# Softmax and product with the values: two transfers taken out of the branches, and a load of 128 partitions cut into 104 and 24

## The chip, the cores and the metric

The kernel runs on one core of a Trainium2 chip. The metric is the device time of one execution in microseconds (us). A core has five engines with an instruction stream each: PE (TensorE, matrix products), DVE (VectorE), ACT (ScalarE), POOL (GpSimd) and SP (SyncE, which here issues every transfer). Transfers between the chip's memory and the core's on-chip memory are carried by 16 DMA engines. Engines wait for each other, and for transfers, by counting semaphores.

## The reference

```python
scores: (8, 12, 1024, 1024) float32      v: (8, 12, 1024, 64) float32
scores_max = np.max(scores, axis=-1, keepdims=True)
attn = np.exp(scores - scores_max)
attn = attn / (np.sum(attn, axis=-1, keepdims=True) + 1e-8)
return np.matmul(attn, v).astype(np.float32)
```

There are 96 heads. Each has 4 MB of scores, 256 KB of values and 256 KB of results.

## The kernel before, in words

A head is 1024 rows of scores. Each of the 128 partitions holds 8 of them, so one load of a head is 128 x 32 KB. The kernel works on *groups* of four heads (`AHEAD = 4`) in a loop of 24 turns, with one buffer of scores (`s_bufs`) for each head of a group. For each head k and each row r = 0 to 7:

- ACT takes the exponential of two rows at a time (L256, no maximum is subtracted). The last two rows of head 3 go one by one. So a head is four ACT instructions, head 3 is five.
- PE transposes the row in eight blocks of 128 x 128 (L268), and DVE copies the result out of PE's accumulator memory (L274, `pt`).
- Two rows later (`LAG = 2`) `finish` multiplies the transposed row with the values on PE (L146). The values carry a column of ones, so the sum of the exponentials comes out beside the product. After four or eight rows `normalise` divides on DVE: a reciprocal (L125) and two products (L130) into `out_sb`. Because of the lag the last rows of a head are finished when the next head's first rows are through; after head 3 the rest is finished at once.

The values of a whole group are loaded as one transfer of 1 MB (`load_v`, L195), cast to half precision by POOL (`cast_v`, L202), and spread by DVE with 16 small copies for a group (`spread_v`, L206) into the tiles that PE reads: four at the start of the group for head 0, and twelve behind the copies of heads 0 and 1, for heads 1 to 3. The results of two heads are stored as one transfer of 512 KB (`store`, L162).

SP issues the transfers in the order of the program. `queue` chains them, so none overtakes another, and each waits first for what it needs: a load of scores for ACT to be done with the buffer, a store for DVE, a load of values for POOL. Before the loop there are the values of the first group, the scores of its four heads, and the values of the second group (L294). In the loop, turn n0 loads the scores of the next group. Load 0 (head 0 of the next group) stands in the loop's body with a condition. Everything else stands at the end of the body in `last` (L215), which has three branches:

- all groups but the last two: load 1, `short` (16 partitions of 4 bytes, into a tile that nothing reads), store 0 (heads 0 and 1), load 2, the values of the group after the next, load 3, store 2 (heads 2 and 3);
- the last group but one: load 1 in two halves, store 0, load 2 in two halves, a quarter of load 3, store 2, the other three quarters;
- the last group: the two stores.

A transfer signals its end on a semaphore. The framework that the kernel is written in has eight for transfers, and gives them to a program's transfers in turn, 0 to 7 and again, as they stand in the program; a full transfer adds 16. In the first branch load 1 has number 1, `short` 2, store 0 number 3, load 2 number 4, the values 5, load 3 number 6, store 2 number 7. In the second branch the halves of load 1 have 1 and 2, store 0 has 3, the halves of load 2 have 4 and 5, the first quarter of load 3 has 6, store 2 has 7, and the other quarters have 0, 1 and 2. Load 0 always has 0. All three branches must leave each semaphore at the same count, since a wait in the next turn names one number for all. Where a branch has fewer transfers on a semaphore than another, SP adds the missing 16 itself, after a wait that all earlier counts on it are in. In the first branch SP does that for number 1 ahead of load 1, for number 2 ahead of `short`, and for number 0 at the end of the branch.

Of the kernel before, what the change touches and what calls it, by code (L numbers as in the profile page):

```python
# [8 lines left out]
FP32 = mybir.dt.float32  # L9
# [5 lines left out]
def kernel(  # L15
# [6 lines left out]
    nc = tc.nc  # L22
    P = 128
# [4 lines left out]
    BH = B * H  # L28
    assert SQ % P == 0 and SK % P == 0
    R = SQ // P  # L30
# [5 lines left out]
    AHEAD = 4  # L36
    Q = P // AHEAD
    S = P // Q
    L = 4
    T = 2  # L40
# [7 lines left out]
    v_bh = v.rearrange("b h (i t) d -> (b h i) (t d)", i=Q)  # L48
# [6 lines left out]
    sb_pool = ctx.enter_context(tc.tile_pool(name="sbpool", bufs=1))  # L55
# [7 lines left out]
        out=order16[:].rearrange("p (t j) -> p t j", t=T),  # L63
        in_=ident32[:].rearrange("p (j t) -> p t j", t=T),
# [13 lines left out]

    s_bufs = buffers(sb_pool, AHEAD, [P, R, SK], FP32, "s_nat")
    v_sb = sb_pool.tile([P, C // L, S, L, D], FP32, name="v_sb")  # L80
    short = sb_pool.tile([16, 1], FP32, name="short")
    v_half = sb_pool.tile([P, C // L, S, L, D], FP16, name="v_half")
    p_bufs = buffers(sb_pool, 8, [P, EB, SK], FP16, "p_nat")
    pt_bufs = buffers(sb_pool, 4, [P, SK], FP16, "pt")
# [9 lines left out]
    def take(bufs):  # L94
        k = turn.get(id(bufs), 0)
        turn[id(bufs)] = k + 1
        return bufs[k % len(bufs)]
# [4 lines left out]
    def after(a, b):  # L102

        tc.add_manual_dep(
            a.ins,
            b.ins.name,
            mybir.DependencyInfo(mybir.DependencyClass.NoSync, mybir.DependencyReason.DATA),
            reason="order",
        )

    def queue(dma):

        if queued:
            after(dma, queued[-1])
        queued.append(dma)

    def one(bh, n):
        return bh[bass.ds(n, 1)].rearrange("o p r d -> (o p) r d")

    def normalise(k, st, first, last):  # L120

        psO = psO_whole if k % 2 == 0 else psO_banks[first]
        psO = psO[:, :, 0 : G * M].rearrange("p b (g m) -> p b g m", m=M)
        recip = st["recip"][:, first:last]
        nc.vector.reciprocal(out=recip, in_=psO[:, :, :, D : D + 1])  # L125
        h = k % T
        for t in range(T):
            part = slice(t * W, (t + 1) * W)
            rows = st["out_sb"][h * W : (h + 1) * W, t, first * G : last * G, :]
            nc.vector.tensor_tensor(  # L130
                out=rows.rearrange("j (b g) d -> j b g d", g=G),
                in0=psO[part, :, :, 0:D],
                in1=recip[part].to_broadcast([W, last - first, G, D]),
                op=mybir.AluOpType.mult,
            )

    def finish(u):

        n0, k, r, pt, st = u
        b, g = r // G, r % G  # L140
        if r == 0:
            st["recip"] = take(rc_bufs)
            st["out_sb"] = out_bufs[k // T]
        bank = psO_whole[:, b] if k % 2 == 0 else psO_banks[b][:, 0]
        for c in range(C):
            nc.tensor.matmul(  # L146
                out=bank[:, g * M : (g + 1) * M],
                lhsT=pt[:, c * P : (c + 1) * P],
                rhs=st["vones"][:, c, 0:M],
                start=(c == 0),  # L150
                stop=(c == C - 1),
            )
        if k % 2 == 1:
            if g == G - 1:
                normalise(k, st, b, b + 1)
        elif r == R - 1:
            normalise(k, st, 0, R // G)

    def store(n0, k):

        rows = out_bh.rearrange("(m x) y -> m x y", x=P)
        dma = nc.sync.dma_start(  # L162
            out=rows[bass.ds((n0 + k) // T, 1)].rearrange("o x y -> (o x) y"),
            in_=out_bufs[k // T][:].rearrange("x t r d -> x (t r d)"),
        )
        for other in stores:
            apart(dma, other)
            apart(other, dma)
        apart(dma, dma)
        stores.append(dma)  # L170
        queue(dma)
# [3 lines left out]
    def apart(dma, other):  # L175
        tc.declare_no_dep(
            dma.ins, other.ins, across_iterations=True, reason="stores of two heads are disjoint"
        )

    def load(k, n, parts=(R,), r=0, **cond):  # L180
        for rows in parts:
            queue(
                nc.sync.dma_start(
                    out=s_bufs[k][:, r : r + rows, :],
                    in_=one(sc_bh, n)[:, r : r + rows, :],
                    **cond,
                )
            )
            r += rows

    def load_v(n):

        rows = v_bh.rearrange("(m x) y -> m x y", x=P)
        queue(
            nc.sync.dma_start(  # L195
                out=v_sb[:].rearrange("x h s l d -> x (h s l d)"),
                in_=rows[bass.ds(n // AHEAD, 1)].rearrange("o x y -> (o x) y"),
            )
        )
# [4 lines left out]
    def spread_v(k, s, behind=None):  # L204

        copy = nc.vector.tensor_copy(  # L206
            out=vones_bufs[k][s * Q : (s + 1) * Q, :, 0:D].rearrange(
                "i (h l) d -> i h l d", l=L
            ),
            in_=v_half[k * Q : (k + 1) * Q, :, s],  # L210
        )
        if behind is not None:
            after(copy, behind)

    def last(n0):  # L215

        before = queued[-1:]

        with tc.If(n0 < BH - 2 * AHEAD) as cmp:
            queued[:] = before
            load(1, (n0 + (AHEAD + 1)) % BH)
            queue(nc.sync.dma_start(out=short[:], in_=v_bh[0:16, 0:1]))
            store(n0, 0)
            load(2, (n0 + (AHEAD + 2)) % BH)
            load_v((n0 + 2 * AHEAD) % BH)
            load(3, (n0 + (AHEAD + 3)) % BH)
            store(n0, T)
        with cmp.Else():  # L230
            with tc.If(n0 < BH - AHEAD) as cmp2:  # L231
                queued[:] = before
                load(1, BH - 3, (4, 4))
                store(n0, 0)
                load(2, BH - 2, (4, 4))
                load(3, BH - 1, (2,))
                store(n0, T)
                load(3, BH - 1, (2, 2, 2), 2)
            with cmp2.Else():
                queued[:] = before  # L240
                store(n0, 0)
                store(n0, T)

    def heads(n0):

        for k in range(AHEAD):
            if k == 0:
                for s in range(S):
                    spread_v(k, s)
            st = dict(vones=vones_bufs[k])  # L250
            for r in range(R):
                if r % EB == 0:
                    p_nat = take(p_bufs)
                    rows = 1 if k == AHEAD - 1 and r == R - EB else EB
                    for g in range(0, EB, rows):
                        nc.scalar.activation(  # L256
                            out=p_nat[:, g : g + rows, :].rearrange(
                                "p r (x v) -> p x r v", v=Q * L
                            ),
                            in_=s_bufs[k][:, r + g : r + g + rows, :].rearrange(  # L260
                                "p r (i x l) -> p x (r i) l", i=Q, l=L
                            ),
                            func=EXP,
                        )
                p_row = p_nat[:, r % EB, :].rearrange("p (h q l) -> p h l q", q=P, l=L)
                psT = take(psT_bufs)
                for c in range(C):
                    nc.tensor.transpose(  # L268
                        out=psT[:, c * P : (c + 1) * P],
                        in_=p_row[:, c // L, c % L, :],  # L270
                        identity=order16[:],
                    )
                pt = take(pt_bufs)
                copy = nc.vector.tensor_copy(out=pt[:], in_=psT[:])  # L274

                if k < 2 and r < 6:
                    spread_v(1 + (k * 6 + r) // S, (k * 6 + r) % S, copy)
                if k == 0 and r == R - 1:
                    load(0, (n0 + AHEAD) % BH, cond=n0 < BH - AHEAD)
                pending.append((n0, k, r, pt, st))  # L280
                if len(pending) > LAG:
                    finish(pending.pop(0))
        while pending:
            finish(pending.pop(0))
        cast_v()
        last(n0)

    assert AHEAD == 4 and T == 2 and R == 8
    assert BH % AHEAD == 0 and BH >= 2 * AHEAD and SK == Q * S * C
    load_v(0)  # L290
    for k in range(AHEAD):
        load(k, k)
    cast_v()
    load_v(AHEAD)  # L294
    with tc.For_i(0, BH, AHEAD, iteration_sync="reg_based") as n0:
        queued.clear()
        heads(n0)
# [30 lines left out]
```

## Time and profile before

| What | Value |
|---|---|
| median of three timed runs | 1087.0 us (1086.9 to 1087.21) |
| profiled execution | 1086.9 us, span from first to last instruction 1085.1 us |
| PE, DVE, ACT, POOL busy | 740.3, 786.5, 735.6, 48.1 us |
| exponentials of two rows (L256) | 408 instructions with the single rows, 704.8 us |
| copies of transposed rows (L274) | 768, 516.8 us, 686 ns each |
| spreads of the values (L206) | 384, 109.5 us, 285 ns each |
| casts of the values (L202) | 25, 47.4 us, 1896 ns each |
| DMA moved | 453.05 MB, mean 418 GB/s over the span |
| a load of scores, from issue to landing | 36.1 us median |
| mean granted clock of PE | 0.828 |

The span counts from the first instruction to the last; what lies around it makes the 1.8 us up to the execution's own time. In the page's slices each digit is the busy share of a fortieth of the span, in tenths. A row of a timeline gives the start, the length, the engine, the line and form, and, in brackets, how long the engine had been idle before it and what released it.

### The profile page before, as it was taken

To read this page: it belongs to the slowest core of one execution; us is meant where nothing else is said; L and a number is where in the kernel's file an instruction comes from. 1 tells how busy PE (TensorE), PEld (TensorE's weight loads), DVE (VectorE), ACT (ScalarE), POOL (GpSimd) and SP (SyncE) were. 2 spreads that over 40 slices of the span, in tenths; PEclk is the share of its full clock that TensorE was granted. 3 is DMA by queue.
4 is the path that set the end of the run, shared out by engine and by line. 5 is a ranking of instruction groups with operands and counts; after the bars stand their busy time and mean duration, and the time that the engine had idled before them with its cause. 6 is when DMAs were issued, how large, how long until landed. Compare 5 with 4: busy or idle time off the path is not lost. (4 is left out here: it accounts for less than half of the span.)

```text
span 1085.1 us, 32113 instructions
## 1 busy us (share of the span) xinstructions
PE 740.3 (68%) x12288; PEld 687.1 (63%) x12288; DVE 786.5 (72%) x1589; ACT 735.6 (68%) x432; POOL 48.1 (4%) x31
## 2 busy tenths in 40 slices
PE   2756776776767667768676767686766767766725
PEld 2756666666667666667676666676666666666625
DVE  3776876876868768678687686786876968768627
ACT  3766685866667767667677676685866666857625
POOL 0000000000000000000000000000000000000000
PEclk9887888878888888788888887888888878888768
DMA  9999999999999999999999999999999999999970
GB/s 405 424 420 427 432 436 426 436 431 429 432 435 424 443 428 432 435 427 430 440 425 436 432 428 429 438 428 438 429 429 440 426 435 434 428 436 434 422 302 39
DMA packets 25619, 453.05 MB, mean 418 GB/s; under 512 B 3472, under 2 KB 3472, under 8 KB 9616
## 3 DMA queue, kind: packets, MB, share of 16 engines
q1 hardware_dynamic: 25616, 453.00, 97.3%
q8 instruction: 3, 0.05, 0.0%
HBM read 432.01 MB, written 25.17 MB: 421 GB/s over the span
## 5 line engine op out<-in xcount | busy, mean ns | idle before, releaser
L256 ACT ACTIVATE p_nat<-s_nat 128x2048 f16<-128x2048 f32 (+1 forms) x408 | 704.8, 1800 | 246.8 <-DMA s_nat<-in_scores_dram 201.7
L268 PE MATMUL psT<-order,p_nat 128*128 128x128 f16 x6144 | 581.2, 248 | 273.4 <-ACT p_nat L256 269.7
L274 DVE COPY pt<-psT 128x1024 f16<-128x1024 f16 x768 | 516.8, 686 | 227.5 <-PE psO_whole L146 86.8
L268 PEld LDWEIGHTS <-p_nat 128*128 128x128 f16 x6144 | 451.9, 123 | 297.3 <-ACT p_nat L256 297.2
L146 PEld LDWEIGHTS <-pt 128*128 128x128 f16 x6144 | 307.5, 109 | 94.7 <-DVE pt L274 93.6
L146 PE MATMUL psO<-vones,pt 128*128 128x65 f16 x3072 | 183.6, 205 | 60.4 <-DVE pt L274 59.2
L146 PE MATMUL psO_whole<-vones,pt 128*128 128x65 f16 x3072 | 189.3, 211 | 5.0 <-DVE pt L274 3.9
L206 DVE COPY vones<-v_half 32x512 f16<-32x512 f16 x384 | 109.5, 285 | 23.0 <-POOL v_half L202 5.9
L202 POOL CAST v_half<-v_sb 128x2048 f16<-128x2048 f32 x25 | 47.4, 1896 | 1014.9 <-DMA v_sb<-in_v_dram 951.3
L256 ACT ACT_TABLE_LOAD x24 | 30.8, 1283 | 89.7 <-DMA s_nat<-in_scores_dram 81.7
L130 DVE TENSOR_TENSOR out_sb<-psO,recip 64x256 f32<-64x256 f32 x192 | 81.1, 423 | 6.0
L130 DVE TENSOR_TENSOR out_sb<-psO_whole,recip 64x512 f32<-64x512 f32 x96 | 66.0, 688 | 3.0
L125 DVE RECIPROCAL recip<-psO 128x4 f32<-128x4 f32 x96 | 17.4, 181 | 32.5 <-PE psO L146 17.6
L125 DVE RECIPROCAL recip<-psO_whole 128x8 f32<-128x8 f32 x48 | 9.7, 203 | 0.8
L71 DVE MEMSET vones<- 128x16 f16 x4 | 0.2, 72 | 0.8 <-PEq L312 0.8
L62 DVE CAST order<-ident 128x128 f16<-128x128 f32 x1 | 0.2, 227 | 0.4 <-POOL ident masks.py:199 0.4
masks.py:199 POOL TENSOR_SCALAR_AFFINE_SELECT ident<-ident 128x128 f32<-128x128 f32 x1 | 0.3, 293 | 0.1
masks.py:197 POOL MEMSET ident<- 128x128 f32 x1 | 0.2, 205 | 0.3 <-POOLq L312 0.3
L312 POOL MEMSET const-float32-0.0<- 128x1 f32 x1 | 0.1, 99 | 0.2 <-issue 0.2
L312 POOL MEMSET const-bfloat16-1.0<- 128x1 bf16 x1 | 0.1, 102 | 0.0
L312 POOL MEMSET const-uint8-127<- 128x1 uint8 x1 | 0.1, 102 | 0.0
L312 POOL MEMSET const-float32-1.0<- 128x1 f32 x1 | 0.1, 99 | 0.0
## 6 DMA issues: line engine op xcount, KB each, us to landing
s_nat<-in_scores_dram SPq DMA_DIRECT2D x94, 4096.0 KB, 36.1
v_sb<-in_v_dram SPq DMA_DIRECT2D x24, 1024.0 KB, 36.9
out_dram<-out_sb SPq DMA_DIRECT2D x48, 512.0 KB, 26.8
s_nat<-in_scores_dram SPq DMA_DIRECT2D x4, 2048.0 KB, 35.3
s_nat<-in_scores_dram SPq DMA_DIRECT2D x4, 1024.0 KB, 24.4
short<-in_v_dram SPq DMA_DIRECT2D x22, 0.1 KB, 35.7
```

Source lines behind the costliest of these rows:

```text
L62: nc.vector.tensor_copy(out=order16[:].rearrange("p (t j) -> p t j", t=T), in_=ident32[:].rearrange("p (j t) -> p t j", t=T),)
L71: nc.vector.memset(vo[:, :, D : D + 2], 1.0)
L125: nc.vector.reciprocal(out=recip, in_=psO[:, :, :, D : D + 1])
L130: nc.vector.tensor_tensor(out=rows.rearrange("j (b g) d -> j b g d", g=G), in0=psO[part, :, :, 0:D], in1=recip[part].to_broadcast([W, last ...
L146: nc.tensor.matmul(out=bank[:, g * M : (g + 1) * M], lhsT=pt[:, c * P : (c + 1) * P], rhs=st["vones"][:, c, 0:M], start=(c == 0), stop=(c ...
L202: nc.gpsimd.tensor_copy(out=v_half[:], in_=v_sb[:])
L206: copy = nc.vector.tensor_copy(out=vones_bufs[k][s * Q : (s + 1) * Q, :, 0:D].rearrange("i (h l) d -> i h l d", l=L), in_=v_half[k * Q : ( ...
L256: nc.scalar.activation(out=p_nat[:, g : g + rows, :].rearrange("p r (x v) -> p x r v", v=Q * L), in_=s_bufs[k][:, r + g : r + g + rows, :] ...
L268: nc.tensor.transpose(out=psT[:, c * P : (c + 1) * P], in_=p_row[:, c // L, c % L, :], identity=order16[:],)
L274: copy = nc.vector.tensor_copy(out=pt[:], in_=psT[:])
L312: nc = _bacc.Bacc("TRN2", target_bir_lowering=False, num_devices=1)
```

## The change

Load 1 and store 0 leave the branches. Load 1 now stands in the loop's body with a condition, as load 0 does, behind the last row of head 1 (`load_next`); store 0 is issued from `finish` when head 1 is done. `short` is gone. In the branch of the last group but one, load 3 comes in pieces of 4, 2, 1 and 1 rows, with the store behind the first piece, and load 1 comes whole. The twelve spreads of a group go behind every second row of heads 0, 1 and 2. The second load of values, ahead of the loop, becomes two transfers: partitions 0 to 103, and 104 to 127. The numbers of the transfers' semaphores change with the order of the program: load 0 has 0, load 1 has 1, store 0 has 2; in the first branch load 2 has 3, the values 4, load 3 has 5, store 2 has 6; in the second the halves of load 2 have 3 and 4, the first piece of load 3 has 5, store 2 has 6, and the other pieces have 7, 0 and 1; in the third store 2 has 3. What SP has to add by itself in the first branch (on 0, 1 and 7) now stands at its end.

```diff
--- before.py
+++ after.py
@@ -78,7 +78,6 @@
 
     s_bufs = buffers(sb_pool, AHEAD, [P, R, SK], FP32, "s_nat")
     v_sb = sb_pool.tile([P, C // L, S, L, D], FP32, name="v_sb")
-    short = sb_pool.tile([16, 1], FP32, name="short")
     v_half = sb_pool.tile([P, C // L, S, L, D], FP16, name="v_half")
     p_bufs = buffers(sb_pool, 8, [P, EB, SK], FP16, "p_nat")
     pt_bufs = buffers(sb_pool, 4, [P, SK], FP16, "pt")
@@ -155,6 +154,8 @@
                 normalise(k, st, b, b + 1)
         elif r == R - 1:
             normalise(k, st, 0, R // G)
+        if r == R - 1 and k == T - 1:
+            store(n0, 0)
 
     def store(n0, k):
 
@@ -212,34 +213,32 @@
         if behind is not None:
             after(copy, behind)
 
+    def load_next(k, n0):
+
+        if k < AHEAD - 2:
+            load(k, (n0 + (AHEAD + k)) % BH, cond=n0 < BH - AHEAD)
+
     def last(n0):
-
 
 
         before = queued[-1:]
 
         with tc.If(n0 < BH - 2 * AHEAD) as cmp:
             queued[:] = before
-            load(1, (n0 + (AHEAD + 1)) % BH)
-            queue(nc.sync.dma_start(out=short[:], in_=v_bh[0:16, 0:1]))
-            store(n0, 0)
-            load(2, (n0 + (AHEAD + 2)) % BH)
+            load(AHEAD - 2, (n0 + (2 * AHEAD - 2)) % BH)
             load_v((n0 + 2 * AHEAD) % BH)
-            load(3, (n0 + (AHEAD + 3)) % BH)
-            store(n0, T)
+            load(AHEAD - 1, (n0 + (2 * AHEAD - 1)) % BH)
+            store(n0, AHEAD - T)
         with cmp.Else():
             with tc.If(n0 < BH - AHEAD) as cmp2:
                 queued[:] = before
-                load(1, BH - 3, (4, 4))
-                store(n0, 0)
-                load(2, BH - 2, (4, 4))
-                load(3, BH - 1, (2,))
-                store(n0, T)
-                load(3, BH - 1, (2, 2, 2), 2)
+                load(AHEAD - 2, BH - 2, (4, 4))
+                load(AHEAD - 1, BH - 1, (4,))
+                store(n0, AHEAD - T)
+                load(AHEAD - 1, BH - 1, (2, 1, 1), 4)
             with cmp2.Else():
                 queued[:] = before
-                store(n0, 0)
-                store(n0, T)
+                store(n0, AHEAD - T)
 
     def heads(n0):
 
@@ -272,11 +271,10 @@
                     )
                 pt = take(pt_bufs)
                 copy = nc.vector.tensor_copy(out=pt[:], in_=psT[:])
-
-                if k < 2 and r < 6:
-                    spread_v(1 + (k * 6 + r) // S, (k * 6 + r) % S, copy)
-                if k == 0 and r == R - 1:
-                    load(0, (n0 + AHEAD) % BH, cond=n0 < BH - AHEAD)
+                if k < AHEAD - 1 and r % (R // S) == 0:
+                    spread_v(k + 1, r // (R // S), copy)
+                if r == R - 1:
+                    load_next(k, n0)
                 pending.append((n0, k, r, pt, st))
                 if len(pending) > LAG:
                     finish(pending.pop(0))
@@ -285,13 +283,19 @@
         cast_v()
         last(n0)
 
-    assert AHEAD == 4 and T == 2 and R == 8
     assert BH % AHEAD == 0 and BH >= 2 * AHEAD and SK == Q * S * C
     load_v(0)
     for k in range(AHEAD):
         load(k, k)
     cast_v()
-    load_v(AHEAD)
+
+
+    for part in (slice(0, 104), slice(104, P)):
+        queue(
+            nc.sync.dma_start(
+                out=v_sb[part].rearrange("x h s l d -> x (h s l d)"), in_=v_bh[P : 2 * P][part]
+            )
+        )
     with tc.For_i(0, BH, AHEAD, iteration_sync="reg_based") as n0:
         queued.clear()
         heads(n0)
```

## The prediction, made before the result was known

> **What bounds the kernel now.** I read the page's slices first, then busy time by stretches, then ScalarE's timeline and waits, SP's issues, and last the trace's records of single packets and completions.
>
> ```profile
> span 1085.1 us, 32113 instructions
> DMA  9999999999999999999999999999999999999970
> GB/s 405 424 420 427 432 436 426 436 431 429 432 435 424 443 428 432 435 427 430 440 425 436 432 428 429 438 428 438 429 429 440 426 435 434 428 436 434 422 302 39
> q1 hardware_dynamic: 25616, 453.00, 97.3%
> ```
>
> The sixteen DMA engines are full until about 1050 us; then they stand nearly idle for 35. Up to there only bytes per engine count; behind it the length of the tail does. The tail by stretches (columns: stretch, its length, busy time of PE, weight load, DVE, ACT, POOL, granted clock, DMA share, GB/s):
>
> ```profile
> 45.00:1005.00 960.00, 676.41 (x11230) 627.76 (x11228) 719.37 (x1451) 674.16 (x396) 43.62 (x23) 0.83 1.01 432
> 1029.70:1050.30 20.60, 3.55 (x60) 3.42 (x57) 4.07 (x8) 0.00 (x0) 0.00 (x0) 0.58 0.97 413
> 1050.30:1072.20 21.90, 17.31 (x316) 15.78 (x317) 17.12 (x34) 21.84 (x13) 1.90 (x1) 0.88 0.08 31
> ```
>
> For 20.6 us ScalarE does nothing while the loads run on; then it works 21.84 us without a pause while they don't. Compute that should have lain beside the last loads follows them. ScalarE's timeline (start, length, form, count, idle before and its releaser):
>
> ```profile
> 1010.12 7.42 ACT L256 ACTIVATE p_nat<-s_nat 128x2048 f16<-128x2048 f32 x5 [4.75 <-DMA s_nat<-in_scores_dram]
> 1021.03 1.28 ACT L256 ACT_TABLE_LOAD   x1 [3.49 <-DMA s_nat<-in_scores_dram]
> 1022.33 7.32 ACT L256 ACTIVATE p_nat<-s_nat 128x2048 f16<-128x2048 f32 x4
> 1050.31 21.84 ACT L256 ACTIVATE p_nat<-s_nat 128x2048 f16<-128x2048 f32 x13 [20.67 <-SPq L323]
> ```
>
> And its waits (total, times, longest):
>
> ```profile
> ACT p_nat L256 <- SPq L323: 44.9, 22, 20.7
> ```
>
> So 21 of these waits share 24.2 us (1.15 each, released with a landing), and one is 20.7: the last group's head 1. The completion records tell on what. The loads of that group land at (latest engine): load 0 1020.94; the halves of load 1 1025.78 and 1030.62; of load 2 1036.83 and 1041.68; the quarters of load 3 1044.10, 1047.78, 1050.21, 1052.63. Head 1 had its data at 1030.6, yet started 0.1 us after 1050.21: the third quarter of load 3. In the built program that quarter (second-last branch) shares semaphore 1 with load 1, and the wait of head 1 asks for the full 32 counts of a group on it, since in the first branch SP adds the spare 16 ahead of load 1's own. The stall is a shared counter, not missing data.
>
> **The change, part by part.**
>
> *Load 1 leaves the branches.* On semaphore 1 its 16 are now the first of each group; ScalarE's wait in the built program asks for 32n+16, where it asked for 32(n+1). The last row of load 3 also counts there, but second. The stall of 20.67 us goes. Late next is the data itself. In order, from the landings above: load 1 whole at 1030.6; head 1 runs 7.32 to 1038.0; head 2 has its first half since 1036.8, its second at 1041.7, just when two activations of about 1.83 are through, and ends at 1045.4. Load 3's first piece is now four rows: 1041.68 + 4.85 (what halves of load 2 are apart) = 1046.53. Behind it: store 1.24, two rows 2.44, one row 1.22, one row 1.22 (half of 2.43 each): the end at 1052.7. Head 3 starts at 1046.6 and takes 7.42; its rows 4 to 7 have landed at 1050.2, 1051.4, 1052.7, before they are needed (1050.3, 1052.1, 1053.1). So only the first piece holds it.
>
> *From head 3's start to the end.* VectorE's rows of the group before, whose head 3 started at 1010.12 with all data there, and those of the end:
>
> ```profile
> 1013.61 0.69 DVE L274 COPY pt<-psT 128x1024 f16<-128x1024 f16 x1 [4.45 <-PE psO_whole L146]
> 1023.83 0.88 DVE L130 TENSOR_TENSOR out_sb<-psO,recip 64x256 f32<-64x256 f32 x2
> 1079.56 0.88 DVE L130 TENSOR_TENSOR out_sb<-psO,recip 64x256 f32<-64x256 f32 x2
> ```
>
> 1023.83 + 0.88 - 1010.12 = 14.6 us from the first exponential to the last product. In the old tail, where ScalarE ran ahead, the same stretch from the first copy was 1070.37 to 1080.44 = 10.1, against 1013.61 to 1024.71 = 11.1; that 1.0 is the lower bound's gain. I take 14.6, as ScalarE is again fed piece by piece. From the last product to the span's end: 1085.1 - 1080.44 = 4.66 (store issued, landed at 1083.13, closing). Unchanged.
>
> *The second load of values.* An 8 KB packet takes 309 ns, starting about 3 ns before its forerunner ends: 8 x 0.306 = 2.45 us per engine and load. With three engines empty, thirteen share 128 packets; ten instead of eight on the fuller ones: +0.61 us. The trace shows no transfer of 104 partitions; bounds are 0 (as now) and 2.45 (the same again on some engine). I take 0.6, nearest to the count of packets. What it can bring: from 60 us on, three of the sixteen completions of every transfer come 2.3 to 2.5 us behind the other pack, after three 16 KB packets of the instruction queue at 27.1, 36.7 and 47.5 us (0.88 to 0.97 each). If those are the uppermost engines, they lose 2.45 and fall in with the rest. But a fourth engine, 0.5 late at 68 us, loses some 0.11 per group in the first store's packets and is last at the end: 2.88 behind the first at 1052.63, while the three are 2.27 to 2.41. The latest decides a landing, so the cut gains nothing unless that drift goes too. I keep the drift: gain 0, bound -2.4 (the pack ends at 1050.2).
>
> [...]
>
> *The 64 byte load goes*: 22 times a data packet and a completion packet of 9 ns on each engine, about 12 ns net of overlaps: -0.26.
>
> *Store 0 and load 1 issued outside the branch.* SP's order stays load 0, load 1, store 0, load 2, values, load 3, store 2; a skipped issue (0.34) in the last group is new. New on SP: at the end of each first branch it waits for load 1 of the same group. In the group before the last branches, head 0's exponentials end at 941.9, so load 0 went out at 942.18; load 1 landed at 943.1. So load 0 goes out 1.0 later, and behind it on SP all else. Cover: what is still queued then (load 2, values, load 3, store 2: 9.7 + 2.45 + 9.7 + 1.24 = 23 us). Cost 0. Without the cover it would be 22 x 1.0.
>
> *Spreads of the values* (384 x 285 ns, same number): 12 per group now behind every second copy of heads 0 to 2. The last comes about 2 us after head 2's exponentials; the cast (1.90) follows it rather than the landing, and the load of values behind the cast goes out some 3.3 later than the 0.69 after load 2 seen at 962.55 and 963.24. Load 3 waits for head 3's exponentials (973.86) anyway; under the same 23 us: 0. VectorE is 75% busy in the steady stretch, so the moved copies hide too.
>
> **Sum.** Head 3 starts at 1046.53 + 0.6 - 0.26 + 0.05 = 1046.9; + 14.6 = 1061.5; + 4.66 = 1066.2 span, 18.9 less. The profiled execution took 1086.9 for its span of 1085.1 (+1.8) and stands 0.1 under the median: 1066.2 + 1.8 = **1068.0**.
>
> **The rivals.**
> 1. *The drift goes as well* (its cause may be the three late engines). The pack alone then sets the landings: 1068.0 - 2.4 = 1065.6. For it: the lag grows only in one store per group. Against: it grew at the same pace at 0.5 late as at 2.2. 25%.
> 2. *The stall stays*: ScalarE or VectorE still waits for a whole counter, now ended by the last row at 1052.7. The old tail of 32.5 us behind the last landing gives 1087.3. Against: the count in the built program. 4%.
> 3. *Slower*: the new wait at the branch's end outlasts the queue. It decides when SP is held over 23 us past load 1's landing, that is if it has to wait for the group's last store. Then each of 22 groups starts on empty engines, at 2.35 (the first load took 4.8 us from issue for 2.45 of packets): +52, 1120. Against: it names load 1. 4%.
> 4. *Another wait takes part of the stall* (store 0's buffer, a late piece): 5 to 12 us of the 20.7 come back, 1073 to 1080. 7%.
>
> My forecast itself: 60%.
>
> **How the numbers follow.** Cases 0 and 1 hold 85%. Their bounds: 1065.6 less 1.0 (VectorE dense) and a little, 1064; 1068.0 plus 1.9 (split at its upper bound) and 2 for the tail's pieces, 1072. Some of that 85 lies outside: 8 in 10 inside. About 0.2%, 2 us, is what a measurement tells from no change: slower 5% (rival 3 and a little), same 4% (rival 2), faster 91%.
>
> **What would show it.** ScalarE: no idle of 20 us near 1030; head 1 of the last group starts at about 1031, released by its load; the last load lands within 3 us of 1052.7; the last product at 1061.5; 14.6 from head 3's start. Completions: three engines no longer 2.3 late. Wrong if ScalarE waits on a semaphore that SP raises, if the DMA row shows slices under 9 before 1040, or if the tail behind the last landing is much over 13 us.

## The result and the profile after

The changed kernel takes 1069.39 us (median; 1069.25 to 1070.48), the kernel before 1086.95 in the same comparison: a ratio of 0.9841 with a 95% interval of 0.9823 to 0.9858, 17.6 us less. The prediction was 1068.0 in a range of 1064 to 1072. The profiled execution took 1069.4, its span 1067.6, predicted 1066.2.

The page of the changed kernel, in the lines that were shown of the kernel before:

```profile
span 1067.6 us, 32186 instructions
DMA  9999999999999999999999999999999999999995
GB/s 393 380 431 433 432 432 432 428 436 431 434 432 432 432 432 432 432 432 429 435 431 433 432 432 432 428 436 431 433 432 432 432 430 433 432 432 429 435 431 215
q1 hardware_dynamic: 24777, 453.00, 99.1%
```

The engines are full until 1055 us and nearly idle for 12, no longer for 35. The second slice is slower than before (380 against 424); that comes back below. The first is too (393 against 405), but it is as low with the second load of values whole (394), so the cut has no part in it. Busy time by stretches of the same kernel (stretch, length, busy time of PE, weight load, DVE, ACT, POOL, granted clock, DMA share, GB/s):

```profile
45.00:1005.00 960.00, 668.53 (x11177) 619.79 (x11176) 717.10 (x1444) 671.44 (x395) 41.65 (x22) 0.84 1.01 431
1033.00:1049.20 16.20, 13.20 (x251) 11.47 (x247) 15.12 (x32) 14.66 (x9) 0.00 (x0) 1.00 0.99 423
1049.20:1062.40 13.20, 8.80 (x176) 7.69 (x176) 11.97 (x24) 7.51 (x5) 1.89 (x1) 0.95 0.33 136
```

The steady stretch is as it was. In the last group compute now lies beside the loads, and the busiest engine there is VectorE, at 15.12 of 16.2 us. ScalarE's timeline at the end:

```profile
1023.53 1.28 ACT L255 ACT_TABLE_LOAD   x1 [3.48 <-DMA s_nat<-in_scores_dram]
1024.82 7.32 ACT L255 ACTIVATE p_nat<-s_nat 128x2048 f16<-128x2048 f32 x4
1033.21 10.93 ACT L255 ACTIVATE p_nat<-s_nat 128x2048 f16<-128x2048 f32 x6 [1.07 <-DMA s_nat<-in_scores_dram]
1049.19 7.63 ACT L255 ACTIVATE p_nat<-s_nat 128x2048 f16<-128x2048 f32 x5 [1.12 <-DMA s_nat<-in_scores_dram]
```

Head 1 of the last group waits 1.07 us and is released by its own load; the wait of 20.67 is gone. So it is in ScalarE's waits, whose longest behind SP is now 1.1:

```profile
ACT p_nat L255 <- SPq L226: 23.7, 22, 1.1
```

VectorE's last row puts the last product's end at 1062.42:

```profile
1061.54 0.88 DVE L129 TENSOR_TENSOR out_sb<-psO,recip 64x256 f32<-64x256 f32 x2
```

The trace's completion records give the rest: the last row of load 3 lands at 1055.35, where the last quarter of load 3 of the kernel before landed at 1052.63. The end of the loads comes 2.7 us later, although no more bytes are moved.

### The profile page after: what moved, and what is told of

Its sections match the earlier page's. It is cut to its first block, busy times and chain, and to the rows that moved or that the text cites. A ratio compares the mean times of both kernels' runs of the same rounds, so it can differ in the third digit from the quotient of the medians.

```text
span 1067.6 us, 32186 instructions
## 1 busy us (share of the span) xinstructions
PE 731.7 (69%) x12288; PEld 677.4 (63%) x12288; DVE 786.5 (74%) x1589; ACT 735.7 (69%) x432; POOL 48.0 (4%) x31
## 4 chain that ended last, share of the span: by engine, by line
DMA 82%; ACT 12%; issue 3%; ACTq 1%; PE 0%; DVE 0%; SPq 0%; PEld 0%; DVEq 0%
DMA s_nat<-in_scores_dram 82%; ACT p_nat L255 12%; ACTq L255 1%; ACTq L226 0%; ACTq L299 0%; SPq L184 0%; DVE pt L273 0%; PE psO L145 0%; PE psT L267 0%; PEld L267 0%; ACTq L327 0%; DVE out_sb L129 0%; PE psO_whole L145 0%; SPq L196 0%; PEld L145 0%
## 5 line engine op out<-in xcount | busy, mean ns | idle before, releaser
L267 PE MATMUL psT<-order,p_nat 128*128 128x128 f16 x6144 | 574.3, 246 | 270.3 <-ACT p_nat L255 269.5
L267 PEld LDWEIGHTS <-p_nat 128*128 128x128 f16 x6144 | 446.7, 123 | 298.9 <-ACT p_nat L255 296.3
L145 PEld LDWEIGHTS <-pt 128*128 128x128 f16 x6144 | 300.8, 107 | 84.6 <-DVE pt L273 81.2
L145 PE MATMUL psO<-vones,pt 128*128 128x65 f16 x3072 | 176.9, 201 | 55.9 <-DVE pt L273 52.7
L203 POOL CAST v_half<-v_sb 128x2048 f16<-128x2048 f32 x25 | 47.3, 1893 | 1005.4 <-DVE vones L207 957.4
```

Source lines behind the costliest of these rows:

```text
L145: nc.tensor.matmul(out=bank[:, g * M : (g + 1) * M], lhsT=pt[:, c * P : (c + 1) * P], rhs=st["vones"][:, c, 0:M], start=(c == 0), stop=(c ...
L203: nc.gpsimd.tensor_copy(out=v_half[:], in_=v_sb[:])
L267: nc.tensor.transpose(out=psT[:, c * P : (c + 1) * P], in_=p_row[:, c // L, c % L, :], identity=order16[:],)
```

## The experiments

**Is the stall a shared counter?** The kernel before, load 1 still in the branches. Only the last three quarters of load 3 become one transfer, so that no piece of load 3 counts on the semaphore of load 1.

```diff
-                load(3, BH - 1, (2, 2, 2), 2)
+                load(3, BH - 1, (6,), 2)
```

> The kernel before, load 1 still in the branches; only the last three quarters of load 3 of the last group but one are one transfer of six rows, so that no piece of load 3 uses the semaphore of load 1. Theory C (the stall of 20.7 us is a shared counter): head 1 of the last group starts at about 1030.7, released by its own load; the six rows land at 1052.6, their exponentials take 5.6 more, and the products end 6 to 7 behind that, at 1064 to 1065.5; span 1069 to 1070.5, time 1071 to 1072.5. Rival (ScalarE waits for the end of load 3 as such, or for SP): the stall stays and is 2.4 us longer, time 1089.

1071.13 us (1070.65 to 1071.88), ratio 0.9855 (0.9838 to 0.9871): 15.8 us less by changing the pieces of a single load. ScalarE's timeline of this kernel:

```profile
1022.27 18.38 ACT L256 ACTIVATE p_nat<-s_nat 128x2048 f16<-128x2048 f32 x10
1041.79 5.52 ACT L256 ACTIVATE p_nat<-s_nat 128x2048 f16<-128x2048 f32 x3 [1.14 <-PE L268]
1052.86 5.61 ACT L256 ACTIVATE p_nat<-s_nat 128x2048 f16<-128x2048 f32 x4 [5.56 <-DMA s_nat<-in_scores_dram]
```

Head 1 follows head 0 without a gap (load 1 still comes in halves here, so it starts even before the expected 1030.7), and the only long wait is 5.56 for the six rows, which land at 1052.76. All 22 of ScalarE's waits behind SP are gone from its list; its waits for loads of scores number 71, where they numbered 49. The data and SP's order are those of before; what went is the count on one semaphore. That the stall was the shared counter is shown.

**What does the cut of the second load of values cost?** The changed kernel with that load whole, and the kernel before with the cut alone.

```diff
-    for part in (slice(0, 104), slice(104, P)):
-        queue(
-            nc.sync.dma_start(
-                out=v_sb[part].rearrange("x h s l d -> x (h s l d)"), in_=v_bh[P : 2 * P][part]
-            )
-        )
+    load_v(AHEAD)
```

> The changed kernel with the second load of values whole again. Theory S (the cut is what made the loads of scores land 2.7 us later than before, through packets that took 620 ns instead of 309): the packets of that load are back at 309 ns, the last row of load 3 lands at about 1052.4 instead of 1055.35, and the time falls by 2.5 to 3.0, from 1069.4 to 1066.4-1066.9. Rival L (the late landing comes from the third packet of the instruction queue, which now hits an engine of the pack): the last landing stays within 1 us of 1055.3 and the time within 1 us of 1069.4. Rival D (the cut pays, because three late engines are made up for): the time rises above 1070.

1065.59 us (1065.52 to 1066.29), ratio 0.9807 (0.9791 to 0.9824). The last row of load 3 lands at 1052.18. This version is 3.8 us faster than the changed kernel, 0.8 more than the most that was expected, and the fastest of the three.

```diff
-    load_v(AHEAD)
+    for part in (slice(0, 104), slice(104, P)):
+        queue(
+            nc.sync.dma_start(
+                out=v_sb[part].rearrange("x h s l d -> x (h s l d)"), in_=v_bh[P : 2 * P][part]
+            )
+        )
```

> The kernel before with the cut of the second load of values alone. Theory S: ScalarE's stall in the last group stays (some 20 us, ended by the third quarter of load 3), and that quarter lands 2.4 to 3.0 later than 1050.2; time 1089.4 to 1090. Rival D (the cut pays): 1084 to 1086. Rival: it makes no difference, 1086.9 within 0.7.

1089.76 us (1089.55 to 1089.95), ratio 1.0027 (1.0016 to 1.0038): 2.9 more. The stall is there, and its end has moved from 1050.31 to 1053.09:

```profile
1053.09 7.32 ACT L256 ACTIVATE p_nat<-s_nat 128x2048 f16<-128x2048 f32 x4 [20.70 <-SPq L328]
```

So the cut costs 2.9 us in the kernel before and 3.8 in the changed one. Of the 3.8 (3.9 in the spans of the profiled runs), head 3 of the last group accounts for 3.15: it starts at 1049.19, and at 1046.04 with the load whole. The other 0.7 lies behind the last product and comes back below. The mechanism is in the packets: whole, all 128 packets of 8 KB of that load take 309 ns. Cut, half of them take 621 or more, and 32 KB packets of scores that run beside it or just behind it (the last ones of the load before, the first ones of the load after) take up to 2.7 us instead of 1.21. The stretch from 44 to 50 us of the changed kernel (bytes are counted where their packet starts, so a short stretch can overshoot):

```profile
44.00:50.00 6.00, 1.64 (x33) 1.48 (x30) 2.96 (x6) 2.52 (x2) 0.00 (x0) 0.78 1.20 272
```

and of the version with the load whole:

```profile
44.00:50.00 6.00, 4.21 (x93) 3.90 (x90) 4.41 (x9) 4.28 (x3) 1.76 (x1) 1.00 1.13 481
```

272 GB/s against 481, with the engines busy throughout in both.

**Why are the packets of a cut load slow?** Three other cuts in the changed kernel: at 96, at 64, and by columns.

```diff
-    for part in (slice(0, 104), slice(104, P)):
+    for part in (slice(0, 96), slice(96, P)):
```

> The changed kernel with the cut at 96 instead of 104, so that both parts can go over all sixteen engines. Theory M (which partitions an engine gets is what halves the rate of a cut load): packets of the second load of values take about 620 ns again although no engine is empty; the load takes 5 us instead of 2.45; time as e1_whole plus 2.4, 1068.8 to 1069.4. Theory N (the three empty engines run ahead into the next load of scores, and that is what slows the others): packets of 309 ns, time as e1_whole, 1066.4 to 1066.9.

1067.78 us (1067.51 to 1070.45), ratio 0.9833 (0.9817 to 0.985). Median packet 516 ns. The packets are slow although no engine is left out, so theory N falls; but they are faster than the 620 that theory M expected, and the time is 1.0 under its range.

```diff
-    for part in (slice(0, 104), slice(104, P)):
+    for part in (slice(0, 64), slice(64, P)):
```

> The changed kernel with the second load of values cut into 64 and 64 partitions. Theory M (a cut load gives an engine a run of neighbouring partitions, and two engines that write near each other slow each other down; 6 and 2 in a run gave 516 ns, 8 and 2 gave 621): packets of 450 to 650 ns with all sixteen engines carrying the same 64 KB; time 1067.5 to 1069.5. Rival P (it is the odd count, 104 or 96, that costs, and a power of two is free): packets of 309 ns and the time of the whole load, 1065.6 within 0.7.

1068.11 us (1067.58 to 1068.32), ratio 0.9827 (0.9811 to 0.9843). Median packet 626 ns. Its stretch:

```profile
44.00:50.00 6.00, 1.64 (x35) 1.48 (x33) 3.27 (x7) 2.29 (x2) 0.00 (x0) 0.92 1.09 269
```

```diff
-    for part in (slice(0, 104), slice(104, P)):
-        queue(
-            nc.sync.dma_start(
-                out=v_sb[part].rearrange("x h s l d -> x (h s l d)"), in_=v_bh[P : 2 * P][part]
-            )
-        )
+    for part in (slice(0, 1024), slice(1024, 2048)):
+        queue(
+            nc.sync.dma_start(
+                out=v_sb[:].rearrange("x h s l d -> x (h s l d)")[:, part],
+                in_=v_bh[P : 2 * P, part],
+            )
+        )
```

> The changed kernel with the second load of values cut by columns instead of partitions: two transfers of 128 partitions, 4 KB of each. Theory M (a transfer of fewer than 128 partitions is slow because of the partitions that each engine writes): every engine carries 16 packets of 4 KB at the usual 159 ns, 2.5 us together, and the time is that of the whole load, 1065.6 within 0.7. Rival T (any two transfers into this tile in place of one are slow): packets of 250 ns and more, time 1067.5 to 1069.5.

1065.88 us (1065.63 to 1066.42), ratio 0.9809 (0.9793 to 0.9825). Median packet 159 ns for 4 KB, as in the stores, though a quarter of them takes 248 or more. Its stretch:

```profile
44.00:50.00 6.00, 3.83 (x82) 3.52 (x81) 4.07 (x9) 4.25 (x3) 0.88 (x1) 1.00 1.10 415
```

Here two transfers for one, each of 128 partitions, are nearly free. Any of the three cuts by partitions is slow, whether three engines are left out (13 and 12 completions for 104 and 24) or all sixteen take part (16 completions for each part of the other two cuts). Empty engines and odd counts are therefore not the cause. What the slow cuts share is that a transfer covers fewer than 128 partitions; that this costs is shown.

The count of packets then gives the sizes, as an estimate: cut at 104, twelve engines carry ten packets of 575 ns in the mean, 5.7 us where the whole load takes 2.5, so 3.3 more; cut at 64, eight packets of 554 are 2.0 more; cut at 96, eight of 502 are 1.5 more. Against the whole load, the last row of load 3 lands 3.2, 1.9 and 1.9 later.

Why a packet is slow is not shown. That engines which write neighbouring partitions slow each other down, as theory M has it, was the author's guess: no record here names the partitions of an engine. Nor do the records tell the writing side from the reading side, as they don't name the rows of the values that an engine reads, and the cut by columns has packets of 4 KB, not 8.

**The two again, on the chip of the cut by columns.**

> The changed kernel as it is, on the same chip as the cut by columns, so that the two can be compared: 1069.4 within 0.7.

> The changed kernel with the second load of values whole, on the same chip: 1065.6 within 0.7.

1069.55 (1069.03 to 1069.97) and 1065.65 (1065.61 to 1066.23): the difference of 3.9 holds. Head 3 starts at 1049.28 and 1046.04 here, 3.2 apart as before.

**Do the other parts matter?** Both on top of the version with the load whole. First the twelve spreads where they stood before:

```diff
-                if k < AHEAD - 1 and r % (R // S) == 0:
-                    spread_v(k + 1, r // (R // S), copy)
+                if k < 2 and r < 6:
+                    spread_v(1 + (k * 6 + r) // S, (k * 6 + r) % S, copy)
```

> The changed kernel with the second load of values whole, and the twelve spreads of a group where they stood before, behind the first six copies of heads 0 and 1. Theory H (as predicted: where the spreads stand is hidden): 1065.6 within 0.5. Rival V (VectorE catches up ahead of head 2 in the last group, so that four spreads less in head 2 end the tail earlier): 4 x 0.31 = 1.2 less, 1064.4. Rival W (VectorE is behind from head 0 of the last group on, and two more spreads in head 0 push it): up to 0.6 more.

1066.35 us (1066.07 to 1067.04), ratio 0.9812 (0.9796 to 0.9829). 0.7 more than with the load whole, hardly above what can be told. Rival V's gain of 1.2 is excluded; rival W's loss of up to 0.6 is not.

Then the pieces of load 3:

```diff
-                load(AHEAD - 1, BH - 1, (4,))
+                load(AHEAD - 1, BH - 1, (2,))
                 store(n0, AHEAD - T)
-                load(AHEAD - 1, BH - 1, (2, 1, 1), 4)
+                load(AHEAD - 1, BH - 1, (2, 2, 2), 2)
```

> The changed kernel with the second load of values whole, and load 3 of the last group but one in pieces of 2, 2, 2 and 2 rows with the store behind the first, as before, instead of 4, 2, 1, 1. Theory F (only the first piece holds head 3, as the prediction had it): head 3 starts 1.15 earlier, with the end of head 2, and the time falls by about 1.1, to 1064.5. Rival V (in the last group VectorE is the bound, not ScalarE's start): within 0.4 of 1065.6. Rival E (the last piece of two rows lands with the same last byte and leaves ScalarE two rows instead of one behind it): 0.5 to 1.0 more.

1066.05 us (1065.72 to 1066.63), ratio 0.9807 (0.9791 to 0.9823). The first piece lands 2.5 earlier and nothing is gained; theory F falls. ScalarE's timeline of this kernel and all engines from 1023 to 1060 us:

```profile
1030.14 16.51 ACT L255 ACTIVATE p_nat<-s_nat 128x2048 f16<-128x2048 f32 x9 [1.07 <-DMA s_nat<-in_scores_dram]
1047.37 1.92 ACT L255 ACTIVATE p_nat<-s_nat 128x2048 f16<-128x2048 f32 x1 [0.72 <-PE L145]
1049.80 1.91 ACT L255 ACTIVATE p_nat<-s_nat 128x2048 f16<-128x2048 f32 x1 [0.51 <-PE L267]
```

```profile
1023.00:1060.00 37.00, 28.64 (x512) 25.72 (x512) 33.10 (x69) 28.36 (x17) 1.90 (x1) 0.89 0.75 318
```

The ninth activation of the first row is head 3's first; it waits for nothing, and the next two are released by PE, not by a load. VectorE is busy for 33.10 of the 37 us, and from 1035.64 to 1058.10 it has no gap of 0.15 or more. So in the last group VectorE sets the pace, not the start of head 3.

**Which engine drifts, and why?** In every trace one engine loses about 0.1 us per group in the packets of the stores. The result buffers exchanged, with the load whole:

```diff
-            st["out_sb"] = out_bufs[k // T]
+            st["out_sb"] = out_bufs[1 - k // T]
...
-            in_=out_bufs[k // T][:].rearrange("x t r d -> x (t r d)"),
+            in_=out_bufs[1 - k // T][:].rearrange("x t r d -> x (t r d)"),
```

> The changed kernel with the second load of values whole, and the two result buffers exchanged: heads 0 and 1 use the second, heads 2 and 3 the first. It asks where one engine loses about 0.1 us per group. Theory B (it depends on the buffer's place in the on-chip memory): the loss moves from the store of heads 0 and 1 to that of heads 2 and 3. Theory O (it depends on the store's place in the order, behind load 1): it stays with the store of heads 0 and 1. Time 1065.6 within 0.7 either way.

1066.58 in one run. The lag of the engine jumps at the store of heads 0 and 1 by 0.20 and 0.21 in two neighbouring groups (0.647 to 0.848 behind the first, 0.812 to 1.017), with the load whole and buffers as they were by 0.15 and 0.14; smaller jumps lie at the other store in both. Over 15 groups from 240 to 880 us the mean jump at the store of heads 0 and 1 is 0.16 exchanged and 0.15 as they were, at the other store 0.03 and 0.02. So it does not follow the buffer. What makes it is open.

## Why the prediction was right, and where it was off

**The stall** went as predicted and for the reason given: a counter that load 1 shared with a later piece of load 3. The experiment with six rows takes it away without moving load 1 at all. Rivals 2 and 4 fall with ScalarE's waits, whose longest behind SP is 1.1.

**The split was mis-sized.** The step "I take 0.6, nearest to the count of packets" is the term that failed, and its upper bound of 2.45 was too low as well. The count of packets fits: the two parts of the load have 13 and 12 completions, where a load of 128 partitions has 16. At 61.9 us the sixteen completions of one load stand at 0 (one), 1.31 and 1.37, 2.02, 2.58 to 2.78 (eleven) and 4.22 behind the first. With 13 and 12 this reads as three engines spared, two of which have been held up by an instruction packet (0.97 and 0.95 us), one that carries the first part alone and is 0.6 ahead of its neighbours, and twelve that carry both; no record names the engine of a completion, so the reading is an estimate. What was wrong is that each packet kept its 309 ns. The rows of the kernel before could not show it, since all its loads of size span 128 partitions. No run shows the term of 0.6. Measured, the landing moves by 2.79 in the kernel before (1055.42 against 1052.63) and by 3.17 in the changed one (1055.35 against 1052.18), and the time by 2.9 and 3.8 us.

**The gain of the split** was taken as 0, because an engine that drifts is last anyway. It did drift on, from 2.87 behind the first at 68.5 us to 5.33 at 1029.2, the same 0.11 per group as before; rival 1 did not come. One more thing spoiled the compensation: the third instruction packet, at 47.5 us before, came at 51.4, and the engine it held up, the one at 4.22, is by the same reading one of the twelve that were not spared. Whether it had hit one of the three uppermost engines before, as the prediction's "if" asks, no record tells.

**The tail was shorter than its term.** From head 3's first exponential to the last product it took 13.23, not 14.6. The sentence "So only the first piece holds it" failed too: VectorE is dense from head 1 of the last group on, and an earlier first piece brings nothing. The prediction had the faster case as a lower bound only. Its 14.6 came from a group in which VectorE was busy for 8.81 us and PE's granted clock was 0.77 in the mean; in the last group of the changed kernel VectorE is busy for 11.99 of the 13.23 and the clock is 0.95. Which of the two shortens it more, no run tells. In a second run of the same kernel, where VectorE was about 1 us further behind when head 3 started, it took 13.80.

**The closing** took 5.18 instead of 4.66. An instruction packet of 1.28 us at 1062.29 held one engine, and the last store's completions spread over 0.86 us, where they spread over 0.21 before. With the load whole, where that packet comes after the last instruction, the closing took 4.4; this is the 0.7 left over above. In the second run of the changed kernel the packet came after the end too, and the closing took 4.5.

The sum of the misses: head 3 started at 1049.19 instead of 1046.9, +2.3; the tail -1.4; the closing +0.5; together +1.4, which is 1067.6 against 1066.2. Two errors half cancel, so the time was nearer than the steps; that is luck. In the second run the shares are others (+2.4, -0.8 and -0.1) and the span is again 1067.6.

**What was costed at nothing** held. SP's new wait stands in its own queue's waits:

```profile
SPq L226 <- SPq L226: 129.8, 22, 9.2
```

It is longer than thought (5.9 us on average; load 0 of the group before the last went out at 990.78, 2.4 after head 0's exponentials, where the prediction's figures give about 1.2), and yet the steady stretch moves 431 GB/s where it moved 432, so rival 3 is excluded. The later cast, which now waits for the last spread rather than for the landing (23 of POOL's waits, 957.4 us, end with a spread; 23, 951.3 us, ended with the load before), is hidden as well.

## What to carry to other kernels

Where branches of a loop share completion semaphores, a wait in the next turn can ask for the count of the whole turn, as the wait of head 1 did here. Look at which later transfer counts on the same semaphore: here ScalarE started at 1050.31 on data that had landed at 1030.62, and the sign in the profile was an engine idle for 20.67 us whose releaser is a queue, beside a DMA share of 0.97. Before a load is cut by partitions to shift a few packets between DMA engines (0.6 us between neighbours here), time the packets of such a cut: here they took 1.7 to 2 times as long (516 to 626 ns against 309), and most packets of a cut by columns did not (159 ns for 4 KB, as in the stores).

## What was not expected

- A load cut into transfers of fewer than 128 partitions ran at about half the rate: packets of 8 KB took 621 ns (104 and 24 partitions), 626 (64 and 64) and 516 (96 and 32) in the median, against 309 for 128 partitions, and 32 KB packets of the loads beside it took up to 2.7 us instead of 1.21.
- Three instruction packets of 16 KB, 0.9 to 1.0 us each in the kernel before, leave three DMA engines late for the rest of the run: two were 1.4 us behind the pack at 46 us, and all three 2.3 to 2.5 behind the first from 60 us to the end. They don't come at a fixed time: the third came at 47.48 us in the kernel before, and at 51.38 and 49.57 in two runs of the changed one.
- One of sixteen engines lost about 0.1 us per group at the stores in every kernel, some 2 us over the run, whatever else was changed. The cause is open.
